# Squared-ReLU MLP after an attention layer: two phases through DRAM, with a seven-product (Strassen) first matmul, float32

## The chip, the cores and the metric

One core of a Trainium2 chip runs the whole program. The metric is the device time of one execution in microseconds (us); lower is better. The core's engines are TensorE (PE; its weight loads are shown apart as PEld), VectorE (DVE), ScalarE (ACT), GpSimd (POOL) and SyncE (SP). SP and POOL also issue the transfers between DRAM and the on-chip memory (SBUF); matmul results land in eight PSUM banks of 128 partitions by 512 float32.

## The reference

One layer: an attention mixer and then an MLP, on 2048 tokens of width 1024, all float32. The change concerns the MLP alone:

```
x = x + g_m * fox_mixer(h, ...)                       # attention, 16 heads
h = rms_norm(x, norm_mlp) * (1 + sc_f) + sh_f         # h: 2048 x 1024
x = x + g_f * (square(relu(h @ w_mlp_in)) @ w_mlp_out) # 1024 -> 4096 -> 1024
```

## The kernel before

Every float32 product is made of three matmuls on a split of each operand into a high and a low part: `mm3` (L132 to L134) adds hi·hi, hi·lo and lo·hi into one bank. A weight or activation that came from DRAM is therefore split before use: ACT casts it to the high part, DVE subtracts that from the raw tile for the low part. A matmul has 128 x 128 weights and 512 moving columns.

The attention, with the out-projection of the first five row tiles (`early_out`) running beside it, ends at about 1480 us; the instructions up to there are the same in both kernels. Then `out_project` handles row tiles 5 to 15 (a row tile is 128 tokens): 48 matmuls into two banks `py`, `ty` = py x gate on DVE (L784), added to x on POOL (L785), stored as x1 by POOL's queue (L786), and its sum of squares taken on ACT (L788). When four row tiles (512 tokens, a block j) are complete, `mlp_norm` makes their rstd (`rstd_of`, L121 to L127: small operations on DVE, Ln and Exp on ACT) and scales the rows, and `mlp_transpose` transposes them on PE (`xt`, L799), applies the modulation on ACT (L801), splits the result on DVE (L803, L804) and, for blocks 1 to 3, stores it to h2_d. These steps are interleaved as side work of the matmul loops.

The MLP is a loop over the four blocks j. Each block goes through eight chunks of four column blocks fb (128 of the 4096 hidden units each). For each fb: load 512 KB of w1 (L876, SP queue) and split it (L864, L865), 24 matmuls into `pu`, ReLU on ACT (L886), square on POOL (L887), split of the result `a` (L889, L890), load 512 KB of w2 and split it. After four fb: 96 matmuls `my` in eight banks of four products each, each bank copied or added to `ya` in SBUF by DVE (L907, L915). In the last chunk of a block DVE multiplies by the second gate and adds (L910, L911), after POOL has multiplied `ya` by the gate and added x1 (L899, L900). So every block reads all of w1 and w2 again, and the hidden activations never leave SBUF.

Where an engine's order matters: each engine, and SP's queue of transfers, works through its instructions in one fixed order. An instruction whose inputs are not ready holds everything behind it on that engine. The program text is not that order: a scheduler interleaves the engines' lists when the program is built.

Of the kernel before, what the change touches and what calls it, by code (L numbers as in the profile page):

```python
# [56 lines left out]
def fox_layer(ctx, tc, x, c, norm_mix, norm_mlp, w_ada, b_ada, w_mlp_in, w_mlp_out,  # L58
# [17 lines left out]
    h2_d = [[dram.tile([P, 2, TJ], F32, name=f"h2_d{j}_{k}") if j else None for k in range(KB)] for j in range(NJ)]  # L76
# [37 lines left out]
    modf = con.tile([P, 2, KB], F32, name="modf")  # L114

# [27 lines left out]
    pw, wo, wo_stage = None, [], []  # L143

# [30 lines left out]
    with ExitStack() as st:  # L175
# [521 lines left out]
        for n, (need, dp) in enumerate(attention()):  # L697
# [29 lines left out]
    sb = ctx.enter_context(tc.tile_pool(name="p2", bufs=2, reuse_waits="tile"))  # L727

    def ring(tag, shape, dt, nm):
        if tag == "w":  # L730
            return pw.tile(shape, dt, tag=tag, name=nm, bufs=8)
        return sb.tile(shape, dt, tag=tag, name=nm,
                       bufs={"raw": 4, "h": 8, "a": 8, "ya": 2, "s": 4, "g": 2}[tag])

    xj, ssj = {}, {}

    def open_x(j):
        xj[j] = ring("ya", [P, RB, D], F32, f"x2_{j}")
        ssj[j] = sb.tile([P, RB], F32, tag="ss", name=f"ss2_{j}", bufs=2)

    def early_load(i):
        j, t = divmod(i, RB)
        nc.sync.dma_start(xj[j][:, t, :], x1_d[i])
        jk = ring("s", [P, D], BF16, f"jk2_{i}")
        nc.scalar.activation(jk, xj[j][:, t, :], AF.Square, accum_out=ssj[j][:, t:t + 1])

    ots = {}

    def out_fetch(i):
        j, t = divmod(i, RB)  # L750
        if t == 0:
            open_x(j)
        ots[i] = ring("raw", [P, D], F32, f"o2_{i}")
        nc.sync.dma_start(ots[i], o_d[i])
        nc.sync.dma_start(xj[j][:, t, :], x[i * P:(i + 1) * P, :])

    def out_load(i):

        if i not in ots:
            out_fetch(i)  # L760
        ot = ots.pop(i)
        oT = []
        for hf in range(2):
# [5 lines left out]
            nc.scalar.copy(a[:, 0, :], pt)  # L769
            nc.vector.tensor_tensor(a[:, 1, :], pt, a[:, 0, :].bitcast(F32), op=ALU.subtract)  # L770
            oT += [(a[:, 0, blk[k]], a[:, 1, blk[k]]) for k in range(4)]
        return oT

    def out_project(i, oT, side):
        j, t = divmod(i, RB)
        xt = xj[j][:, t, :]
        for hf, cs in enumerate(halves):
            py = psS.tile([P, TJ], F32, tag="S", name=f"py{i}_{hf}")
            for kb in range(KB):
                mm3(py, oT[kb], (wo[kb][:, 0, cs], wo[kb][:, 1, cs]), kb == 0, kb == KB - 1)  # L780
                if kb % 4 == 3:
# [29 lines left out]
    h2_first = []

    def load_hT(j):
        hT = []
        for kb in range(KB):
            r = ring("h", [P, 2, TJ], F32R, f"m_h{j}_{kb}")
            nc.sync.dma_start(r.bitcast(F32), h2_d[j][kb])
            hT.append((r[:, 0, :], r[:, 1, :]))
        return hT

    def run(q):
        if q and next(q[0], None) is None and q[0].gi_frame is None:
            q.pop(0)

    side, soon = [], []
    for j in range(NEARLY // RB + (NEARLY % RB > 0)):
        open_x(j)
    oT = out_load(NEARLY)
    out_fetch(NEARLY + 1)
    gates = []  # L830
    for r in range(2):
        g = ring("g", [P, D], F32, f"gate_bc{r}")
        nc.sync.dma_start(g, gate_d[r:r + 1, :].broadcast_to([P, D]))
        gates.append(g)
    gm, gf = gates
# [111 lines left out]
```

## Time and profile before

| | us |
|---|---|
| median of 3 runs (3119.01 to 3124.51) | 3119.08 |
| the profiled execution | 3121.49 |
| span of the profile | 3119.8 |
| PE busy (share of the span) | 2870.4 (92%) |
| DVE busy | 1930.7 (62%) |
| ACT busy | 1433.1 (46%) |
| POOL busy | 1040.5 (33%) |
| mean granted TensorE clock | 0.966 of full speed |
| moved by DMA, mean over the span | 161 GB/s |

The span runs from the first to the last instruction; the profiled execution took 1.7 us more than its span. "Busy" is the time in which an engine executes; the granted clock is the share of TensorE's full speed (2.4 GHz) that it was allowed. Matmuls overlap in the records (each is shown with about 0.4 us, but one starts every 0.23 us), so counts in a stretch say more than their durations.

### The profile page before, as it was taken

What the parts mean: (1) busy time and instruction counts of PE and PEld (TensorE: products, weight loads), DVE (VectorE), ACT (ScalarE), POOL (GpSimd) and SP (SyncE); (2) the same over time, 40 slices, a digit from 0 to 9 for tenths busy, and PEclk for the clock granted to TensorE, in tenths of its full rate; (3) what the DMA queues carried; (4) which work ended last, traced back from release to release, by engine and by line L of the source; (5) the groups of instructions that cost most, each with busy time, mean ns of one, the idle gap of its engine ahead of it and who ended that gap; (6) DMA issues with size and microseconds to landing.
All of it is one profiled execution on the core that took longest, in us unless ns stands there. A gap on an engine that the chain in (4) does not pass through costs nothing.

```text
span 3119.8 us, 44614 instructions
## 1 busy us (share of the span) xinstructions
PE 2870.4 (92%) x16587; PEld 2375.9 (76%) x16587; DVE 1930.7 (62%) x3319; ACT 1433.1 (46%) x2267; POOL 1040.5 (33%) x811
## 2 busy tenths in 40 slices
PE   4788889888988898988999999999999999999999
PEld 4667777777877777776788888788887888878887
DVE  6688978988888877878356433443335333453334
ACT  4466766666676767766233322232222223222321
POOL 3354545545464645445332100410013001311103
PEclk9799989999999999998999999999999999999999
DMA  8479999999999989979755432543235323352332
GB/s 274 124 174 208 208 193 218 209 204 208 213 209 211 201 191 197 189 163 211 215 191 200 132 93 80 172 138 95 75 108 203 94 81 108 95 192 91 108 94 69
DMA packets 852122, 502.34 MB, mean 161 GB/s; under 512 B 585396, under 2 KB 782076, under 8 KB 851904
## 3 DMA queue, kind: packets, MB, share of 16 engines
q1 hardware_dynamic: 843536, 469.60, 62.1%
q0 software_dynamic: 8368, 29.89, 2.5%
q8 instruction: 130, 2.13, 0.3%
q14 instruction: 88, 0.72, 0.1%
HBM read 310.50 MB, written 46.28 MB: 114 GB/s over the span
## 4 chain that ended last, share of the span: by engine, by line
PE 49%; DVE 1%; DMA 1%; ACT 0%; issue 0%; SPq 0%; POOL 0%; DVEq 0%; ACTq 0%
PE my L134 8%; PE my L132 7%; PE my L133 7%; PE pu L134 7%; PE pu L132 7%; PE pu L133 7%; PE py L132 1%; PE py L133 1%; PE py L134 1%; DVE w L865 1%; DMA w1r<-in_w_mlp_in_dram 1%; PE xt L799 0%; PE e_py L132 0%; DMA pT<-ph 0%; PE e_py L134 0%; PE e_py L133 0%
## 5 line engine op out<-in xcount | busy, mean ns | idle before, releaser
L574 DVE SCALAR_TENSOR_TENSOR ph<-L,ph 128x1024 f16<-128x1024 f32 (+7 forms) x384 | 438.3, 1152 | 81.2 <-ACT ph L562 79.5
L887 POOL TENSOR_TENSOR rl<-rl 128x512 f32<-128x512 f32 x128 | 139.1, 1086 | 1024.6 <-ACT rl L886 1019.7
L864 ACT CAST w<-w1r 128x1024 fp32r<-128x1024 f32 x128 | 133.5, 1043 | 598.6 <-PE my L134 553.5
L132 PE MATMUL my<-w,a 128*128 128x512 f32 x1024 | 405.0, 396 | 0.1
L133 PE MATMUL my<-w,a 128*128 128x512 f32 x1024 | 402.9, 394 | 0.0
L134 PE MATMUL my<-w,a 128*128 128x512 f32 x1024 | 395.9, 396 | 2.9 <-DVE a L890 2.9
L562 ACT ACTIVATE ph<-L 128x1024 f16<-128x1024 f32 (+7 forms) x384 | 301.7, 804 | 177.4 <-DMA pT<-ph 152.6
L407 POOL TENSOR_TENSOR hl<-hl,hh 128x1024 fp32r<-128x1024 f32 x120 | 299.5, 2497 | 243.7 <-ACT hh L406 205.4
L487 PE MATMUL psq<-w,hh 128*128 128x384 f32 (+1 forms) x960 | 343.5, 359 | 26.5 <-DVE v L496 12.5
L489 PE MATMUL psq<-w,hl 128*128 128x384 f32 (+1 forms) x960 | 354.4, 371 | 3.2 <-POOL hl L407 2.9
L544 DVE CUSTOM_DVE_ANT_0 L<-S,F 128x1024 f32<-128x1024 f32 (+7 forms) x384 | 343.1, 904 | 19.5 <-PE S L538 6.7
L488 PE MATMUL psq<-w,hh 128*128 128x384 f32 (+1 forms) x960 | 342.7, 359 | 6.1 <-POOL w L333 6.1
L555 ACT ACTIVATE L<-L,st 128x128 f32<-128x128 f32 (+15 forms) x256 | 306.7, 1198 | 89.2 <-DVE st L549 84.9
L537 PE MATMUL S<-kT,qT 128*128 128x512 f32 (+3 forms) x640 | 261.8, 411 | 77.4 <-DVE mx L544 66.6
L600 PE MATMUL po<-v,pT 128*128 128x128 f16 x2176 | 277.1, 228 | 55.4 <-DMA pT<-ph 47.0
L865 DVE TENSOR_TENSOR w<-w1r,w 128x1024 fp32r<-128x1024 f32 x128 | 169.9, 1328 | 236.6 <-ACT w L864 236.6
L915 DVE TENSOR_TENSOR ya<-my,ya 128x512 f32<-128x512 f32 x192 | 128.0, 687 | 292.7 <-PE my L134 292.7
L134 PE MATMUL pu<-m_h,w 128*128 128x512 f32 x768 | 304.4, 396 | 0.0
L132 PE MATMUL pu<-m_h,w 128*128 128x512 f32 x768 | 303.8, 396 | 0.0
L133 PE MATMUL pu<-m_h,w 128*128 128x512 f32 x768 | 301.8, 393 | 0.0
L865 DVE TENSOR_TENSOR w<-w2r,w 128x1024 fp32r<-128x1024 f32 x128 | 165.7, 1295 | 203.7 <-ACT w L864 203.7
L600 PEld LDWEIGHTS <-pT 128*128 128x128 f16 x2176 | 205.1, 103 | 86.2 <-DMA pT<-ph 58.3
(214 smaller groups left out, 6115.8 us busy)
## 6 DMA issues: line engine op xcount, KB each, us to landing
w1r<-in_w_mlp_in_dram SPq DMA_DIRECT2D x128, 512.0 KB
w2r<-in_w_mlp_out_dram SPq DMA_DIRECT2D x128, 512.0 KB
hl<-hT_d SPq DMA_DIRECT2D x120, 512.0 KB
F<-nF_d SPq DMA_DIRECT2D x64, 256.0 KB
wa<-in_w_ada_dram SPq DMA_DIRECT2D x32, 512.0 KB
x<-in_x_dram SPq DMA_DIRECT2D x27, 512.0 KB
wr<-in_fox_w_in_dram SPq DMA_DIRECT2D x64, 192.0 KB
h_d<-h2r POOLq DMA_DIRECT2D x24, 512.0 KB, 3.4
```

The source lines that it names most:

```text
L132: nc.tensor.matmul(ps, lhsT=a[0], rhs=b[0], start=first, stop=False)
L133: nc.tensor.matmul(ps, lhsT=a[0], rhs=b[1], start=False, stop=False)
L134: nc.tensor.matmul(ps, lhsT=a[1], rhs=b[0], start=False, stop=last)
L487: nc.tensor.matmul(ps[:, :n], lhsT=hh, rhs=w[:, 0, :n], start=(kb == 0), stop=False)
L488: nc.tensor.matmul(ps[:, :n], lhsT=hh, rhs=w[:, 1, :n], start=False, stop=False)
L489: nc.tensor.matmul(ps[:, :n], lhsT=hl, rhs=w[:, 0, :n], start=False, stop=(kb == KB - 1))
L544: nc.vector.tensor_tensor_reduce(out=L[:, c0:c1], in0=s2[:, :c1 - c0], in1=Fb[g, h, cch // 2][:, :c1 - c0], scale=1.0, scalar=-3.0e38, op0 ...
L555: nc.scalar.activation(L[:, :W], L[:, :W], AF.Exp, bias=st[:, h:h + 1], scale=1.0, accum_out=st[:, 2 + h:3 + h])
L562: nc.scalar.activation(ph[:, :w], L[:, s0:s0 + w], AF.Copy, scale=PSCALE)
L574: nc.vector.scalar_tensor_tensor(ph[:, w:w + c], L[:, s0:s0 + c], PSCALE, ph[:, :c], op0=ALU.mult, op1=ALU.subtract)
L600: nc.tensor.matmul(po[:, h, :], lhsT=pT[:, bb, :], rhs=v, start=(b == 0), stop=False)
L865: nc.vector.tensor_tensor(w[:, 1, :], raw, w[:, 0, :].bitcast(F32), op=ALU.subtract)
```

## The change

The MLP is done in two phases with the hidden activations written to DRAM in between (a_d), and 1024 tokens (a half s, two blocks j) at a time instead of 512.

Phase 1 computes relu(h @ w1)² in groups of 2x2x2 blocks. A group takes two column blocks (fb = p and p + 16), two halves of the 1024-deep contraction, and two blocks of 512 tokens: eight block products of 4 x 3 matmuls each become seven by Strassen's identity (the Winograd form). The job X of a pair p has the products P1 and P2, the job Y has P6, P7, P5, P4 and P3. The operands of the seven products are sums and differences: of quarters of w1 (S1 to S4, made on POOL by `stage`, L952) and of blocks of h (T1 to T4, made on POOL in `prep_t`, L803 to L810, once for each half s and each of four contraction blocks kk). All are split as before (`split`, L750 on ACT and L751 on DVE; ht0 and ht1 are the raw T1 and T2). The results are combined by DVE additions (`finish`, L980, and `partial`, L987), P1 is first copied out of PSUM by ACT (L999); `finish` then does ReLU on ACT (L981) and the square on POOL (L982), and SP stores the tile (256 KB) to a_d (L1024, L1040). Every operand is prepared three products ahead (LOOK = 3); the first four and the last four X jobs of a half stand together ahead of the four Y jobs.

Phase 2 multiplies a_d by w2: for each half s eight chunks of four fb; a w2 block is loaded (L1069) once for 1024 tokens, the activations are read back (L1075) and split, and 192 matmuls per chunk go to banks that DVE adds to `ya` (L1110 onwards, as before).

Ahead of phase 1, the out-projection now makes the rstd of every row tile by itself (`row_rms`, L756 and L757), transposes only row tiles 0 to 7 (`turn`, from L764), and stores the unsplit h to h2_d by SP's queue; `prep_x` loads and splits the two operands that are not sums (B00, B10). The transposes of the other eight row tiles (with x1 read back, L900) run inside the first half of phase 1. The buffers of the out-projection are given up ahead of phase 1, and those of phase 1 ahead of phase 2, so the new tiles lie in memory that the old ones have used.

```diff
-    for j in range(NJ):
-        hT = load_hT(j) if j > 0 else h2_first
...
+    def row_rms(i, xt):
+        jk = ring("s", [P, D], BF16, f"jk2_{i}")
+        ss = sb.tile([P, 1], F32, tag="ss", name=f"ss2_{i}", bufs=2)
+        nc.scalar.activation(jk, xt, AF.Square, accum_out=ss)
+        nc.vector.tensor_copy(rs2[:, i:i + 1], rstd_of(sb, ss, 1.0 / D, 1, f"x2_{i}"))
...
+    def prep_t(s):
+        for kk in range(KH):
+            b00, b01, b11, b10 = [load_h(s, k, t, kk) for k, t in ((0, 0), (0, 1), (1, 1), (1, 0))]
+            t1, t2 = [ring("hs", [P, TJ], F32, f"ht{n}_{s}_{kk}") for n in range(2)]
+            nc.gpsimd.tensor_tensor(t1, b01, b00, op=ALU.subtract)
+            nc.gpsimd.tensor_tensor(t2, b11, t1, op=ALU.subtract)
+            keep("T2", s, kk, t2)
+            keep("T1", s, kk, t1)
+            yield
+            nc.gpsimd.tensor_tensor(b01, b11, b01, op=ALU.subtract)
+            keep("T3", s, kk, b01)
+            nc.gpsimd.tensor_tensor(b10, b10, t2, op=ALU.subtract)
+            keep("T4", s, kk, b10)
+            keep("B11", s, kk, b11)
+            yield
...
+    RING = {"raw": 8, "w": 5, "st": 5, "p1": 6, "u": 4, "c": 4, "hs": 8}
...
+    PROD = {"P1": ("A00", "B00"), "P2": ("A01", "B10"), "P6": ("S2", "T2"), "P5": ("S1", "T1"),
+            "P7": ("S3", "T3"), "P4": ("A11", "T4"), "P3": ("S4", "B11")}
...
+        if prod == "P6":
+            stage(job, "S1", ALU.add, raw["A10"], raw["A11"])
+            stage(job, "S2", ALU.subtract, job.ops["S1"], raw["A00"])
+            used(job, "A10", "A11", "A00")
+        elif prod == "P7":
+            stage(job, "S3", ALU.subtract, raw["A00"], raw["A10"])
+            stage(job, "S4", ALU.subtract, raw["A01"], job.ops["S2"])
...
+    def finish(job, f, t, ps, other):
+
+        s, p = job.s, job.p
+        c = ring("c", [P, TJ], F32, f"c{f}{t}_{s}_{p}")
+        nc.vector.tensor_tensor(c, ps, other, op=ALU.add)
+        nc.scalar.activation(c, c, AF.Relu)
+        nc.gpsimd.tensor_tensor(c, c, c, op=ALU.mult)
+        late.append((a_d[2 * s + t][p + f * FP], c))
...
+        for kk in range(KH):
+            mm3(ps, (w[:, 0, blk[kk]], w[:, 1, blk[kk]]), hop[b, s, kk], kk == 0, kk == KH - 1)
...
+    for n, (job, prod) in enumerate(slots):
+        while len(late) > 1:
+            nc.sync.dma_start(*late.pop(0))
+        load_jobs()
+        if n + LOOK < len(slots):
+            prepare(*slots[n + LOOK])
+        multiply(job, prod)
+        run(aux)
...
+    for d, c in late:
+        nc.sync.dma_start(d, c)
+    s1x.close()
+    hxx.close()
...
+    RING = {"wr": 2, "ar": 4, "w": 8, "a": 12, "ya": 10, "gf": 1, "x1": 2, "s": 2}
...
+                if t == 0:
+                    wr = ring("wr", [P, D], F32, f"w2r{s}_{fb}")
+                    nc.sync.dma_start(wr, w2[fb * P:(fb + 1) * P, :])
+                    w = ring("w", [P, 2, D], F32R, f"w2_{s}_{fb}")
+                    split(w, wr)
...
+                ar = ring("ar", [P, TJ], F32, f"ar{s}_{fb}_{t}")
+                nc.sync.dma_start(ar, a_d[2 * s + t][fb])
```

The change moves instructions on every engine. Three places follow, each with the rows of one engine in their order (the numbers at the ends of names only tell instances apart; a row's waits are the engines or transfer queues that must have finished something first).

The first is ACT at the end of the out-projection. Before, behind the last row tile's sum of squares (jk2_15), stand casts of weights and the ReLU of a `pu` bank whose matmuls need nothing of that tile; several weight casts stand ahead of it.

```order
L864 CAST w1_0_2_19226<-w1r0_2_19224 128x1024 [waits DMAHW5_49,PE_49]
L864 CAST w2_0_2_19284<-w2r0_2_19282 128x1024 [waits DMAHW6_49,PE_49]
L788 ACTIVATE jk2_15_19125,ss2_3_18653<-x2_3_18652 128x1024 [waits DMAHW0_49,Activation_49,Pool_49]
L864 CAST w1_0_3_19289<-w1r0_3_19287 128x1024 [waits DMAHW7_49,PE_49]
L122 ACTIVATE t_x2_3_19129<-v_x2_3_19127 128x4 [waits DVE_49]
```

Of the change:

```order
L756 ACTIVATE jk2_15_19357,ss2_15_19358<-x2_15_19209 128x1024 [waits DMAHW7_49,Pool_49]
L127 ACTIVATE t_x2_15_19362<-v_x2_15_19360 128x1 [waits DVE_49]
L128 ACTIVATE y_x2_15_19361<-t_x2_15_19362 128x1 [waits Activation_49]
L750 CAST wP1_0_0_19392<-w1_X0_0_A00_19376 128x512 [waits DMAHW6_49,DMAHW2_49,DMAHW0_49]
L750 CAST wP2_0_0_19395<-w1_X0_0_A01_19378 128x512 [waits DMAHW1_49,PE_49]
```

The first weight cast of phase 1 (wP1) now stands behind the whole chain of the last row tile; before, casts of the MLP stood on both sides of it.

The second is POOL at the start of phase 1, of the change (before, POOL had here one square L887 for each fb and nothing else but transfers).

```order
L952 TENSOR_TENSOR S1_0_0_19588<-w1_Y0_0_A10_19401,w1_Y0_0_A11_19403 128x512 [waits DMAHW1_49,DMAHW0_49,PE_49]
L952 TENSOR_TENSOR S2_0_0_19590<-S1_0_0_19588,w1_Y0_0_A00_19405 128x512 [waits DMAHW2_49,Pool_49]
L952 TENSOR_TENSOR S3_0_0_19624<-w1_Y0_0_A00_19405,w1_Y0_0_A10_19401 128x512
L803 TENSOR_TENSOR ht0_0_0_19433<-hr0_01_0_19427,hr0_00_0_19425 128x512 [waits DMAHW4_49,DMAHW3_49]
L982 TENSOR_TENSOR c00_0_0_19461<-c00_0_0_19461 128x512 [waits PE_49,Activation_49]
L952 TENSOR_TENSOR S4_0_0_19626<-w1_Y0_0_A01_19443,S2_0_0_19590 128x512 [waits DMAHW7_49,Pool_49]
L804 TENSOR_TENSOR ht1_0_0_19434<-hr0_11_0_19429,ht0_0_0_19433 128x512 [waits DMAHW5_49,Pool_49]
L808 TENSOR_TENSOR hr0_01_0_19427<-hr0_11_0_19429,hr0_01_0_19427 128x512
L952 TENSOR_TENSOR S1_0_1_19753<-w1_Y0_1_A10_19476,w1_Y0_1_A11_19514 128x512 [waits DMAHW1_49,DMAHW0_49]
L982 TENSOR_TENSOR c00_0_1_19532<-c00_0_1_19532 128x512 [waits Activation_49]
L810 TENSOR_TENSOR hr0_10_0_19431<-hr0_10_0_19431,ht1_0_0_19434 128x512 [waits DMAHW6_49,Pool_49]
```

All sums and differences of w1 and of h and the squares are one list on POOL; from S1 of the first Y job to the last T4 of the first half this list has 29 rows (25 of two inputs, 4 squares).

The third is SP's queue at the start of phase 2, of the change. (Before, the first loads of a chunk stand between other loads, as in the two last rows.)

```order
L1024 DMA a_d3_31_236<-c11_1_15_24950 128x512 [waits DMAHW5_49,Pool_49]
L1040 DMA a_d2_31_204<-c10_1_15_24968 128x512 [waits DMAHW6_49,Pool_49]
L1040 DMA a_d3_15_220<-c01_1_15_24986 128x512 [waits DMAHW7_49,Pool_49]
L1069 DMA w2r0_0_24997<-in_w_mlp_out_dram 128x1024 [waits DMAHW0_49,PE_49]
L1075 DMA ar0_0_0_25002<-a_d0_0_109 128x512 [waits DMAHW1_49]
L1069 DMA w2r0_1_25007<-in_w_mlp_out_dram 128x1024 [waits DMAHW2_49,PE_49]
L1075 DMA ar0_1_0_25012<-a_d0_1_110 128x512 [waits DMAHW3_49,DVE_49]
L1075 DMA ar0_2_0_25022<-a_d0_2_111 128x512 [waits DMAHW4_49]
L1075 DMA ar0_3_0_25032<-a_d0_3_112 128x512 [waits DMAHW5_49]
L1092 DMA gate_bc1_25057<-gate_d_88 128x1024 [waits DMAHW6_49,PE_49]
L1100 DMA m_x1_0_27055<-x1_d0_89 128x1024 [waits DMAHW7_49,PE_49]
L1100 DMA m_x1_1_27102<-x1_d1_90 128x1024 [waits DMAHW0_49]
L1069 DMA w2r0_2_25017<-in_w_mlp_out_dram 128x1024 [waits DMAHW1_49,DVE_49]
```

```order
L893 DMA w2r0_2_19282<-in_w_mlp_out_dram 128x1024 [waits DMAHW6_49,DMAHW2_49,DVE_49]
L876 DMA w1r0_3_19287<-in_w_mlp_in_dram 128x8x128 [waits DMAHW7_49,DMAHW3_49,DVE_49]
```

The first load of w2 stands behind the store of the very last tile of phase 1, which waits for POOL's square; the third load of w2 stands behind the gate and two loads of x1.

## Rows read from the trace of the kernel before

**Rows 1.** Windows: us, PE busy (matmuls started), granted clock, DMA share, GB/s.
```profile
2000.00:2200.00 200.00, 198.89 (x852) 1.00 0.43 140
2400.00:2600.00 200.00, 200.00 (x859) 1.00 0.34 103
3000.00:3120.00 120.00, 114.92 (x493) 0.99 0.25 79
```
**Rows 2.** Waits from 1480 us on: in total us, times, longest us.
```profile
POOL rl L887 <- ACT rl L886: 1019.7, 119, 27.0
ACT w L864 <- PE my L134: 553.5, 31, 17.9
```
**Rows 3.** Lines from 1480 us on: busy us, mean ns; idle before, releaser.
```profile
L134 PE MATMUL my<-w,a 128*128 128x512 f32 x1024 | 395.9, 396 | 2.9 <-DVE a L890 2.9
...
L889 ACT CAST a<-rl 128x512 fp32r<-128x512 f32 x128 | 79.4, 620 | 46.8 <-POOL rl L887 46.8
L886 ACT ACTIVATE rl<-pu 128x512 f32<-128x512 f32 x128 | 76.5, 597 | 372.9 <-PE pu L134 357.5 <-issue 15.4
```
**Rows 4.** One line's instructions: duration ns min/median/max, first and last start us.
```profile
L865 DVE TENSOR_TENSOR w<-w1r,w x128: 1211/1226/3447, 1669.8 to 3072.0; 128x1024 fp32r<-128x1024 f32 x128
...
L890 DVE TENSOR_TENSOR a<-rl,a x128: 675/679/2231, 1685.5 to 3095.0; 128x512 fp32r<-128x512 f32 x128
...
L915 DVE TENSOR_TENSOR ya<-my,ya x192: 679/691/692, 1753.6 to 3070.3; 128x512 f32<-128x512 f32 x192
...
L887 POOL TENSOR_TENSOR rl<-rl x128: 1031/1040/2046, 1682.2 to 3093.2; 128x512 f32<-128x512 f32 x128
...
L785 POOL TENSOR_TENSOR x<-x,ty x22: 1262/1294/1367, 1551.8 to 1675.2; 128x512 f32<-128x512 f32 x22
```
**Rows 5.** Timeline of DVE, 1985 to 2005 us: start us, duration us.
```profile
1991.30 1.22 DVE L865 TENSOR_TENSOR w<-w2r,w 128x1024 fp32r<-128x1024 f32 x1
1992.43 3.45 DVE L865 TENSOR_TENSOR w<-w1r,w 128x1024 fp32r<-128x1024 f32 x1
1995.80 3.43 DVE L865 TENSOR_TENSOR w<-w2r,w 128x1024 fp32r<-128x1024 f32 x1
```
**Rows 6.** Timeline of POOL, the same stretch.
```profile
1991.46 3.33 POOL L899 TENSOR_TENSOR ya<-ya,gate_bc 128x1024 f32<-128x1024 f32 x1 [3.29 <-DVE ya L915]
1994.76 6.75 POOL L900 TENSOR_TENSOR ya<-ya,m_x 128x1024 f32<-128x1024 f32 x2
```
**Rows 7.** Timeline at the end of the out-projection: DVE, POOL, then ACT.
```profile
1674.46 0.68 DVE L784 TENSOR_TENSOR ty<-py,gate_bc 128x512 f32<-128x512 f32 x1
...
1675.22 1.30 POOL L785 TENSOR_TENSOR x<-x,ty 128x512 f32<-128x512 f32 x1 [5.17 <-DVE ty L784]
...
1678.51 1.05 ACT L788 ACTIVATE jk<-x 128x1024 bf16<-128x1024 f32 x1
1679.47 0.19 ACT L788 ACTIVATION_READ_ACCUMULATOR jk<-x 128x1 f32 x1
...
1680.49 0.20 ACT L122 ACTIVATE t_x<-v_x 128x4 f32<-128x4 f32 x1
```
**Rows 8.** Chain that ended last, two of its pieces: start us, us.
```profile
2719.00 0.32 SPq L898
2719.41 5.17 DMA w1r<-in_w_mlp_in_dram
2724.60 1.06 ACT w L864
```
**Rows 9.** DMA issues: count, KB each, median us from issue to landing.
```profile
h_d<-h2r POOLq DMA_DIRECT2D x24, 512.0 KB, 3.4
...
x_d<-x POOLq DMA_DIRECT2D x11, 512.0 KB, 4.0
...
x_d<-wo_raw POOLq DMA_DIRECT2D x5, 256.0 KB, 5.7
```
**Rows 10.** Windows around a wait of PE, columns as in rows 1.
```profile
1464.00:1466.00 2.00, 0.00 (x0) 0.75 1.17 253
1466.00:1468.00 2.00, 1.94 (x17) 0.50 0.72 135
...
1470.00:1472.00 2.00, 2.00 (x9) 0.54 0.95 257
```
**Rows 11.** Timeline of PE behind that wait.
```profile
1466.06 0.29 PE L600 MATMUL po<-v,pT 128*128 128x128 f16 x1 [3.13 <-DMA pT<-ph]
```

More of the change, by code (lines that the diff above doesn't have):

```diff
@@ L741, in early_load @@
[L741 to L755 removed]
+    NS = NJ // 2
@@ L811, in fox_layer, with early_load @@
[L811 to L823, printed above, removed]
+        row_rms(i, xt)
+    def early_load(i):
+        xt = ring("xe", [P, D], F32, f"x2_{i}")
+        nc.sync.dma_start(xt, x1_d[i])
+        row_rms(i, xt)
+        return turn(i, lambda hf: xt[:, halves[hf]])
@@ L825, in fox_layer, with held_x @@
+    def held_x(xt):
+        return lambda hf: xt[:, halves[hf]]
+    NA = 2 * RB
     side, soon = [], []
[L826 to L828 removed]
+    nxt = out_load(NEARLY)
     out_fetch(NEARLY + 1)
[L830 to L835, printed above, removed]
+    gm = ring("gm", [P, D], F32, "gate_bc0")
@@ L850, in fox_layer, with ring @@
-    side += soon
+        if i < NA:
+            soon.append(turn(i, held_x(xt)))
+        if i == NA:
+            soon.append(prep_x(0))
+    while side:
+        run(side)
+    px.close()
+    pwx.close()
+    s1x = ctx.enter_context(ExitStack())
+    sb = s1x.enter_context(tc.tile_pool(name="p3", bufs=2, reuse_waits="tile"))
+    RING = {"raw": 8, "w": 5, "st": 5, "p1": 6, "u": 4, "c": 4, "hs": 8}
+    RING["hx"] = RING["hs"]
+    def ring(tag, shape, dt, nm):
+        tag = "hs" if tag == "hx" else tag
+        return sb.tile(shape, dt, tag=tag, name=nm, bufs=RING[tag])
@@ new lines, in fox_layer @@
+    LOOK = 3
+    aux = [prep_t(0)] + [turn(i, reload_x(i)) for i in range(NA, NT)]
+    n_last_x = max(n for n, (job, prod) in enumerate(slots) if job.s == 0 and job.kind == "X")
+    n_last_y = max(n for n, (job, prod) in enumerate(slots) if job.s == 0)
+    load_jobs()
+    for n in range(LOOK):
+        prepare(*slots[n])
+    for n, (job, prod) in enumerate(slots):
+        while len(late) > 1:
+            nc.sync.dma_start(*late.pop(0))
+        load_jobs()
+        if n + LOOK < len(slots):
+            prepare(*slots[n + LOOK])
+        multiply(job, prod)
+        run(aux)
+        if n == n_last_x:
+            aux.append(prep_x(1))
+        if n == n_last_y:
+            while aux:
+                run(aux)
+            aux.append(prep_t(1))
+        if n == 2 * Q - 1:
+            while len(aux) > NT - NA:
+                run(aux)
```

313 lines of the change are left out of this document (209 added, 104 removed).

## Prediction

> **What bounds the kernel now.** I read the windows first. From 2000 us on PE is busy practically all the time at full clock [rows 1]; in the fullest window 859 matmuls start in 200.00 us, one every 232.8 ns. That pitch, not the 0.396 us that a record shows [rows 3], is the price of a matmul here. Next the waits: the long ones are other engines waiting for each other or for PE, such as POOL for ReLU, 1019.7 us, or ACT for `my`, 553.5 us [rows 2]. PE itself lost 2.9 us behind `my` [rows 3], and a few us where a block j begins, visible as 198.89 of 200. So in the MLP only the number of matmuls counts, as long as operands come in time, and fewer matmuls shorten the program nearly one to one.
>
> **What is removed.** The first product had 4 x 32 x 24 = 3072 matmuls `pu`; now there are 2 halves x 16 pairs x 7 products x 12 = 2688. The second keeps its 3072, and the transposes keep their number. Saved: 384 x 232.8 ns = **89.4 us**. The waits at `my` inside the fused loop go too, 2.9 us. Together **-92.3 us**.
>
> Beside this goes a check of whether PE stays the bound. A pair of jobs (X and Y) has 84 matmuls, 84 x 0.2328 = 19.56 us. DVE has seven subtractions of 0.68 (as L890) and seven additions out of PSUM of 0.69 (as L915) [rows 4], 9.6 us. POOL has four sums of two inputs at 1.29 (as L785) and four squares at 1.04 (as L887) [rows 4], 9.3 us. ACT has seven casts of 0.62, four ReLU of 0.60 [rows 3] and one copy, about 7.3 us. DMA moves six loads and four stores of 256 KB, 2.5 MB, 134 GB/s over the pair, where the MLP already saw 140 [rows 1]. Each fits under 19.56.
>
> DVE and POOL do not run freely beside each other: a subtraction L865, 1.22 us, took 3.45 and 3.43 while POOL ran L899 and L900 [rows 5], and these took 3.33 and 3.4 [rows 6]; each starts where the other ends. Additions from PSUM (L915) never stretch, maximum 692 ns [rows 4]. So I let POOL and the seven DVE subtractions exclude each other: 9.3 + 4.8 = 14.1 us of 19.56. Steady state stays with PE. The Trainium skill, page "SBUF — State Buffer", section "Who interferes with whom", says that a DVE instruction with two SBUF inputs and a GpSimd instruction that reads SBUF share one port as an exclusive lock, and that DVE with one SBUF input does not contend; it speaks against a change that adds POOL sums, and rows 4 to 6 agree with it.
>
> The Trainium skill, page "TensorE: Matmul & The Clock Gate", section "Wait — 56ns, not 53.3ns?", gives 215.7 ns from start to start at 512 columns; with it the saving would be 82.8 us. The trace's 232.8 ns decides.
>
> **What is added, all of it at the seams.** Before, PE always had matmuls of another kind to go on with. Now three dependencies run through everything.
>
> (A) Out-projection. Each row tile makes its own rstd, about nine small operations where four tiles shared one set, and `run(side)` comes twice as often. Nothing of PE's next tile hangs on it; 0 to 3 us, nearest to nothing: **1**.
>
> (B) Start of phase 1. Once the last `py` is done, wP1 stands on ACT behind the last tile's chain (the first place in the order): `ty` 0.68, POOL's sum 1.30, sum of squares 1.05 + 0.19, one small DVE step, Ln and Exp at 0.20 each [rows 7], then the cast 0.62 [rows 3]: 4.2 us and some 1 us of handovers, 5.3. Before, the matmuls of `pu` covered this. Then PE has eight X products (96 matmuls, 22.3 us) and what the first Y job offers as T operands arrive (60, 14 us, and transposes, 1.8): 38 us of work until T4 of the last kk. POOL's list to there has 25 x 1.26 to 1.29 + 4 x 1.04 = 36 us. It starts late: SP sends the loads of h only after all X and three Y quarters of w1, and the Y quarters reuse tiles that the first splits must free, so about 7 us after the last `py`, plus a landing of 3.4 to 5.7 us [rows 9] for the first difference: at 11. The ring of eight tiles for h lets the loads of kk = 2 and 3 start only when DVE has read older ones: 2 to 3 us idle. So T4 is ready at 50 to 53 us if DVE never shuts POOL out, at up to 68 with full exclusion (some 25 splits of 0.68 fall into the stretch). PE needs it at 5.3 + 38 = 43. Bubble: 5.3 + (8 to 25), that is 13 to 31 us, to 36 with loads as slow as 5.7 each time. Exclusion was seen, so I take the upper middle, **27**.
>
> (C) From the first half to the second. The T operands of the second half go into the buffers of the first, so prep_t(1) comes only behind its last Y product. Cover are the four X jobs ahead, 8 x 2.79 = 22 us; POOL must do about 19 operations, 24 us, plus splits, and the loads. 0 to 12 us; the POOL work alone ends about when the cover does, so I take **6**.
>
> (D) From phase 1 to phase 2. The first w2 load on SP stands behind the last store of a_d (third place): after the last matmul DVE 0.69, ReLU 0.60, square 1.04, handovers: 2.6 us. Then a load of 512 KB, 5.17 us, and its cast, 1.06 [rows 8], the cast of a, 0.62: PE restarts at about 9.4. Then w2 of block 2 stands behind the gate and two x1 loads, in a ring of two, so PE pauses again; below, the second pause vanishes (8 us in all); above, it costs two loads (18). I take **12**.
>
> (E) Clock. After PE had waited 3.13 us [rows 11] the granted clock was 0.50 until about 1472 us [rows 10], some 5.6 us at 1.2 instead of 2.4 GHz, a loss of 2.8. Seams B and D are longer gaps: 2 x 2.8 = **6** (0 to 8).
>
> (F) Small waits in steady state and the last chunk, where POOL multiplies 16 tiles against DVE: 0 to 6, **1**. The end behind the last matmul is the same as before.
>
> Phase 2 costs nothing else: a chunk has 192 matmuls, 44.7 us, against DVE 4 x 1.22 + 8 x 0.68 + 16 x 0.69 = 21.4 us and 4.2 MB of DMA, 94 GB/s.
>
> Sum: -92.3 + 1 + 27 + 6 + 12 + 6 + 1 = **-39 us**. The profiled execution took 3121.5, so 3082; the median of runs lies 2.4 us lower, so I predict **3080 us**. With all low ends (0 + 13 + 0 + 8 + 0 + 0 = 21) it is 3048, with all high ends (3 + 36 + 12 + 18 + 8 + 6 = 83) 3110.
>
> **Rivals.**
> 1. The seams are cheap: T operands keep up (PE's order interleaves the four products as they arrive), C is covered, D restarts once. Costs 21 to 35, time **3048 to 3062**. For it: POOL's bare list (36 us) is shorter than PE's cover. Against: in-order loads and the exclusion of rows 5 and 6. Chance 0.22.
> 2. The seams are long: every stage waits for a load in turn, B and C together 48 or more, D 18, clock 8. Costs 68 to 90, time **3095 to 3117**. For it: SP is one queue. Against: an issue takes SP 0.32 us [rows 8], so loads can be under way side by side. Chance 0.2.
> 3. Slower: the pair's chain of waits sets the pace in phase 1. A product's operand must pass a load, POOL's sum, cast and subtraction within three products, 8.4 us; S1, S2, cast and subtraction alone take 2 x 1.29 + 0.62 + 0.68 = 3.9, and squares queued on POOL and stores on SP stand in between. If PE waits in each pair, 32 pairs multiply it: from 19.56 + 39/32 = 20.8 us a pair on, the gain is gone; at 22 us it is 32 x 2.4 = 78 us more, **3158**. For it: POOL's list mixes squares that wait for PE with sums that PE waits for. Against: 14.1 of 19.56 us of work, 4.5 us of slack in a product's lead. Chance 0.08.
> 4. The program does not have the fewer matmuls or PE's pitch changes. Its order shows 2688; the shapes are the same. Chance below 0.02, put to rival 3.
>
> **Numbers.** Forecast (3062 to 3095) 0.5, rivals 0.22, 0.2, 0.08. The range 3047 to 3111 leaves out the tail of rival 2 and rival 3, and a little below rival 1: about 0.15. A measurement of this kernel tells 0.2 per cent, 6 us, from no change, so faster means below 3112.8: 0.5 + 0.22 + 0.16 = 0.88; same 0.04; slower 0.08.
>
> **What would show it.** Right: 2688 matmuls of the first product at 232.8 ns; PE with three visible gaps, where phase 1 starts, at its half, and where phase 2 starts, of about 32, 6 and 15 us with their clocks at 0.50; between them PE at 99 per cent or more; POOL nearly without idle time in the first 50 us of phase 1; DVE subtractions stretched beside POOL. Wrong: PE idle in every pair (rival 3), or PE waiting there for loads of w1 rather than for T operands (rival 2), or gaps that sum to under 25 us (rival 1).

## The result, and the profile after

| | before | after |
|---|---|---|
| median of 4 runs, us | 3121.80 (3119.01 to 3124.51) | 3043.84 (3041.05 to 3048.27) |
| ratio, 95% interval | | 0.9752 (0.9733 to 0.9770) |
| profiled execution, its span, us | 3121.49, 3119.8 | 3046.07, 3044.4 |
| PE / DVE / ACT / POOL busy, us | 2870 / 1931 / 1433 / 1041 | 2760 / 2078 / 1460 / 1257 |
| matmuls of the first product | 3072 | 2688 |

Faster by 78 us (the 3121.80 are the 3119.08 of the table ahead of the prediction with a fourth run); forecast were 3080 us and a range from 3047 to 3111. The time lies 3 us below the range and 36 below the forecast.

The windows of the kernel after (columns as in rows 1), first two stretches in the middle of the phases, then the seams:

```profile
1900.00:2000.00 100.00, 100.00 (x442) 1.00 0.48 153
2400.00:2600.00 200.00, 200.00 (x884) 1.00 0.28 90
...
1670.50:1740.00 69.50, 54.50 (x179) 0.80 0.57 173
1740.00:2015.00 275.00, 273.83 (x1232) 1.00 0.57 177
2015.00:2045.00 30.00, 22.05 (x81) 0.83 0.54 170
2045.00:2331.90 286.90, 286.90 (x1268) 1.00 0.40 126
2331.90:2350.00 18.10, 10.05 (x35) 0.72 0.84 307
```

The second line is the surprise. In 200 us with PE full and its clock at 1.00 now 884 matmuls start; before, 859 [rows 1]. The `my` matmuls, 3072 of the same shape in both kernels, start every 226.7 ns instead of every 233.3 (the mean over sequences without a gap; the prediction's 232.8 came from dividing 200 us by a count that takes in the matmuls at both edges). This is no wait that has gone: PE was full in both.

The waits of PE from 1660 us on, after (us in total, times, longest us), are the seams that were forecast:

```profile
PE my L137 <- ACT a L750: 8.1, 1, 8.1
PE mP L137 <- DVE c L980: 5.3, 1, 5.3
PE mP L137 <- ACT T L750: 4.7, 4, 2.9
PE mP L137 <- ACT wP L750: 4.5, 1, 4.5
PE mP L138 <- DVE T L751: 3.1, 6, 1.2
PE mP L137 <- ACT p L999: 2.6, 1, 2.6
PE mP L139 <- DVE wP L751: 1.9, 1, 1.9
```

The gaps in PE's timeline after (in brackets: idle before, releaser) tell where three of them stand: start of phase 1, its half, phase 2.

```profile
1675.36 0.50 PE L137 MATMUL mP<-B,wP 128*128 128x512 f32 x1 [4.54 <-ACT wP L750]
...
2033.57 0.80 PE L137 MATMUL mP<-B,wP 128*128 128x512 f32 x1 [5.32 <-DVE c L980]
...
2340.33 2.07 PE L137 MATMUL my<-w,a 128*128 128x512 f32 x4 [8.05 <-ACT a L750]
```

DVE and then POOL of the kernel after, in the first of them (start us, duration us). A subtraction of two SBUF tiles takes 0.68 us by itself [rows 4], a POOL sum 1.27; here they take 1.6 to 1.8. Their records overlap, so a duration contains waiting: a subtraction ends 0.54 to 0.55 us behind the end of a POOL record (1703.07 to 1703.61, 1699.66 to 1700.21), a POOL sum 1.14 to 1.15 us behind the end of a subtraction (1700.21 to 1701.36, 1703.61 to 1704.75). They work in turn. An addition that reads PSUM (L980) keeps its 0.68:

```profile
1698.45 1.76 DVE L751 TENSOR_TENSOR T<-hr,T 128x512 fp32r<-128x512 f32 x1
1700.13 0.68 DVE L980 TENSOR_TENSOR c<-mP,p 128x512 f32<-128x512 f32 x1
...
1702.02 1.59 DVE L751 TENSOR_TENSOR T<-hr,T 128x512 fp32r<-128x512 f32 x1
1703.53 1.77 DVE L751 TENSOR_TENSOR B<-hr,B 128x512 fp32r<-128x512 f32 x1
```

```profile
1697.94 1.72 POOL L810 TENSOR_TENSOR hr<-hr,ht 128x512 f32<-128x512 f32 x1
1699.62 1.74 POOL L952 TENSOR_TENSOR S<-S,w_Y_A 128x512 f32<-128x512 f32 x1
1701.32 1.75 POOL L952 TENSOR_TENSOR S<-w_Y_A,w_Y_A 128x512 f32<-128x512 f32 x1
1703.02 1.73 POOL L803 TENSOR_TENSOR ht<-hr,hr 128x512 f32<-128x512 f32 x1
```

So the account was nearly right, and beside it something had happened that was not in the account: all matmuls of the MLP had become 6.7 ns shorter, 5760 x 6.67 = 38 us.

What could that be? The matmuls of the out-projection (py), of the same shape, still started every 233.5 ns in the kernel after, so neither the chip nor the execution was faster. One of its sequences, 94 steps in 21.95 us:

```profile
1648.48 0.41 PE L138 MATMUL py<-wo,oT 128*128 128x512 f32 x1
...
1670.43 0.39 PE L139 MATMUL py<-wo,oT 128*128 128x512 f32 x1
```

The shapes, the types and the program around a matmul are the same. The tiles had moved, though. The address of a tile within its partition is fixed when the program is built, and it is read from the built program; the traces don't show it. Before, w1, w2 and wo lay at 224 modulo 256 bytes, hT at 64, the activations at 128; after, every operand of the MLP lies at 128. The theory was that the address of the operands sets the pitch, that is, the time from one matmul's start to the next one's. The rivals: the place in memory or PSUM, something in the two-phase order, or the chip.

### The profile page after: what moved, and what is told of

Same layout as the page of the kernel before. It is cut to its first block, busy times and chain, and to the rows that moved or that the text cites. A ratio compares the mean times of both kernels' runs of the same rounds, so it can differ in the third digit from the quotient of the medians.

```text
span 3044.4 us, 45983 instructions
## 1 busy us (share of the span) xinstructions
PE 2760.2 (91%) x16203; PEld 2306.8 (76%) x16203; DVE 2078.0 (68%) x3659; ACT 1460.2 (48%) x2507; POOL 1256.7 (41%) x947
## 5 line engine op out<-in xcount | busy, mean ns | idle before, releaser
L606 PE MATMUL po<-v,pT 128*128 128x128 f16 x2176 | 276.5, 228 | 69.5 <-DMA pT<-ph 61.1
L543 PE MATMUL S<-kT,qT 128*128 128x512 f32 (+3 forms) x640 | 262.3, 411 | 71.0 <-DVE mx L550 62.0
L606 PEld LDWEIGHTS <-pT 128*128 128x128 f16 x2176 | 204.7, 103 | 100.2 <-DMA pT<-ph 71.9
L1101 POOL TENSOR_TENSOR ya<-ya,gate_bc 128x1024 f32<-128x1024 f32 x16 | 41.1, 2572 | 546.2 <-DVE ya L1118 546.1
L607 PE MATMUL po<-v,pT 128*128 128x64 f16 x2176 | 258.7, 200 | 0.0
L544 PE MATMUL S<-kT,qT 128*128 128x512 f32 (+3 forms) x640 | 241.1, 384 | 0.0
L137 PEld LDWEIGHTS my<-w,a 128*128 128x128 f32 x1024 | 192.8, 188 | 49.1 <-ACT a L750 8.5
L607 PEld LDWEIGHTS <-pT 128*128 128x128 f16 x2176 | 197.7, 101 | 42.6 <-issue 31.7
L750 ACT CAST w<-w2r 128x1024 fp32r<-128x1024 f32 x64 | 67.3, 1051 | 336.3 <-PE my L139 264.0
L138 PEld LDWEIGHTS my<-w,a 128*128 128x128 f32 x1024 | 193.0, 188 | 40.2
```

The source lines that it names most:

```text
L137: nc.tensor.matmul(ps, lhsT=a[0], rhs=b[0], start=first, stop=False)
L138: nc.tensor.matmul(ps, lhsT=a[0], rhs=b[1], start=False, stop=False)
L606: nc.tensor.matmul(po[:, h, :], lhsT=pT[:, bb, :], rhs=v, start=(b == 0), stop=False)
L607: nc.tensor.matmul(po[:, h, 0:HD], lhsT=pT[:, nw + bb, :], rhs=v[:, 0:HD], start=False, stop=(b == nb - 1))
```

## The experiments

Where an unused tile is put in, everything behind it moves up in memory; the instructions stay the same. In experiments 1 to 7 this is the only edit (4 to 6 also clear one unused tile). Of experiments 1, 2, 3 and 7 there is one execution each, so there the pitches count and not the totals; of the others there are four.

**1. One operand off.** The T operands, B11 and, in phase 2, the activations move by 32 bytes:

```diff
+            once(sb, "T")
             w = sb.tile([P, 2, TJ], F32R, tag="hT", name=f"{name}_{s}_{kk}", bufs=5 * KH)
...
+                once(sb, "A4")
                 a = ring("a", [P, 2, TJ], F32R, f"a{s}_{fb}_{t}")
```

`once` allocates an unused tile of the given size (here 32 bytes in a partition) at its first call and nothing afterwards.

> The changed kernel with empty gaps in the on-chip memory: in phase 1 the T operands and B11 (moving, 28 of 28 kilobytes of the Y job's operands) lie 32 bytes off a multiple of 128, the weights and B00, B10 on it; in phase 2 the activations (weights of the matmul) lie 32 bytes off, w2 on it. Theory (the start-to-start time of a 512-column matmul depends on the address of its operands: 226.7 ns when both are multiples of 64 bytes, 233.3 ns when one is not): X products stay at 226.7 ns, Y products go to 233.3, `my` to 233.3; time 3044 + (1920 + 3072) x 6.67 ns = 3077 us. Rival 1 (the place in memory, the PSUM bank or the chip sets it, not the alignment): 226.7 everywhere, 3044 us. Rival 2 (only the moving operand's address counts): Y 233.3, `my` 226.7, 3057 us.

Measured: 3072.7 us. X products stay at 226.7 ns, but for the first eight or so behind a Y job, which are mixed; Y products go to 233.2, `my` to 233.3. Within one execution a run of X products is followed by Y products (PE's timeline, starts 0.226 and then 0.233 us apart):

```profile
1901.08 0.39 PE L137 MATMUL mP<-B,wP 128*128 128x512 f32 x1
...
1904.25 0.39 PE L139 MATMUL mP<-B,wP 128*128 128x512 f32 x1
1904.48 0.40 PE L137 MATMUL mP<-T,wP 128*128 128x512 f32 x1
...
1911.48 0.39 PE L137 MATMUL mP<-T,wP 128*128 128x512 f32 x1
```

14 steps from 1901.08 to 1904.25 are 226.4 ns each, 30 steps from 1904.48 to 1911.48 are 233.3. The place and the chip as rivals are out (32 bytes do it, and both pitches stand in one execution), and so is rival 2, since `my` got slow by its weights alone.

**2. Both off, with other gaps** (32 bytes ahead of B00, ahead of the weights of phase 1, and ahead of both operands of phase 2).

> As the run before it, with other gaps: in phase 1 the weights lie 32 bytes off, B00 and B10 too, the T operands on a multiple of 128; in phase 2 both operands lie 32 bytes off. Theory (each operand counts by itself): X, Y and `my` all at 233.3 ns, 3044 + 5760 x 6.67 ns = 3082 us. Rival 1 (place, not alignment): 226.7 everywhere, 3044 us. Rival 3 (only the two operands' offset from one another counts): X and `my` at 226.7, Y at 233.3, 3057 us. The e_py matmuls of both traces (both operands 32 bytes off a multiple of 64, at 232.2 and 228.9 ns) speak for something between.

Measured: 3083.9 us, X, Y and `my` at 233.3 to 233.4. As the first theory said; but the gaps had put the operands at 160 and 32 modulo 256, not on the same offset, so rival 3 was not yet tested. The window of `my`, against 884 in the kernel after:

```profile
2460.00:2660.00 200.00, 200.00 (x859) 1.00 0.30 99
```

**3. Gaps of 64.**

> As the run before it, with gaps of 64 bytes: in phase 1 the weights lie 64 bytes off a multiple of 128, B00 and B10 too, the T operands on it; in phase 2 w2 (moving) lies 64 bytes off, the activations on it. Theory with a grain of 64 bytes: 226.7 ns everywhere, 3044 us. With a grain of 128 bytes: X, Y and `my` at 233.3, 3082 us.

Measured: 3075.6 us, Y 229.2, `my` 233.3. Both grains fail: there are more than two values. Y has moving at 128 and weights at 64; e_py, which was at 229.3 in the kernel after, has 224 and 160, the same distance.

**4. The kernel before, moved.** 96 bytes at the upper end of memory, so that w1, w2 and wo go from 224 to 128 modulo 256:

```diff
+                    padR = ctx.enter_context(tc.tile_pool(name="padR", bufs=1, side="right"))
+                    nc.vector.memset(padR.tile([P, 24], F32, name="pad_R"), 0.0)
                     pw = ctx.enter_context(tc.tile_pool(name="pw", bufs=2, reuse_waits="tile", side="right"))
```

> The kernel before with one edit: an unused 96-byte tile at the upper end of the on-chip memory, so that the weights of w1, w2 and wo, which lay 32 bytes off a multiple of 64, lie on a multiple of 128 (the activations and hT already lie on multiples of 64). Nothing else changes. Theory: `pu`, `my` and `py` at 226.7 ns, 3121.8 - (6144 + 528) x 6.67 ns = 3077 us. Rival 1 (the faster matmuls came from the two phases or from where the new tiles lie): no change, 3122 us, pitch 233.3.

Measured: 3097.3 us, ratio to before 0.9941 (0.9923 to 0.9959), where 3077 was expected. `my` fell to 226.9 and py to 228.5, but `pu` (hT at 64, weights at 128) stayed at 233.3. Half of it, as only one of the two products of the MLP had got operands at the same offset.

**5. The kernel before, all at 128.** The same and 64 bytes ahead of hT.

> The kernel before with the 96-byte gap at the upper end (as in the aligned run before it) and a 64-byte gap ahead of the hT tiles, so that both operands of `pu`, `my` and `py` lie on multiples of 128 bytes. Theory, with the grain corrected to 128 bytes: `pu` goes from 233.3 to 226.7 ns too, 3072 x 6.67 ns = 20.5 us less than the aligned run before it (3097.3), 3077 us; then the change proper, with equal alignment, is worth only 3077 - 3044 = 33 us. Rival (what matters is the rest modulo 512, which was equal, 384, in all fast cases; here hT lies at 128 of 512 and the weights at 384): `pu` stays at 233.3, 3097 us.

Measured: 3083.7 us, ratio 0.9874 (0.9854 to 0.9895), `pu` at 226.7 too. The window of `my` and `pu` in this kernel, against the 859 of rows 1:

```profile
2460.00:2660.00 200.00, 200.00 (x884) 1.00 0.33 100
```

The kernel before, run beside it, took 3119.8, which is 4 us more than beside experiment 4; the rest of the 7 us above the 3077 expected is not explained. So 36 us, against the change's 78, are to be had in the kernel before by two empty gaps, without any of its 384 matmuls less. hT at 128 and weights at 384 modulo 512 are as good as equal, so the period is no longer than 256 bytes.

**6. The kernel after with attention and out-projection moved** (96 bytes at both ends).

> The changed kernel with gaps of 96 bytes at both ends, so that the operands of the attention's and out-projection's matmuls lie on multiples of 128 (some of 64, for head slices) as well; the MLP's lie there already. Theory: py and e_py fall from 233.4 and 229.3 to 226.7 ns, 528 x 6.7 + 240 x 2.6 ns = 4 us; in the attention, where PE is busy 0.87 of the time, 0 to 10 us more; 3030 to 3040 us. Rival (alignment acts only on the MLP's tiles): 3044 us.

Measured: 3026.7 us, ratio to before 0.9694 (0.9674 to 0.9714), 17 us less than the change and below the range expected. py fell to 228 ns (its long sequences to 226.7): from its first matmul to its last it took 136.1 instead of 138.9 us (136.1 again in the two versions below, 138.9 in experiment 9). But e_py went up, from 229.3 to 232.6, with wo at 128 and its weights at 0 modulo 256: multiples of 128, and yet slow. That speaks against "multiples of 128" and for a distance. So only 2 to 3 of the 17 us can be laid to the pitch. Most of the rest was gained ahead of the MLP: the first e_py stands at 1408.8 us, in the kernel after at 1418.8. All four runs (3018.9 to 3030.6) lie below the four of the change, so this is no chance of one execution. The two versions at the end, whose gap at the lower end is 192 bytes instead of 64, did not have it (1419.6 and 1420.4). What made the attention shorter here stays open.

**7. Distance or multiple.** Gaps that set the two readings against each other: Y at 160 and 160, X at 224 and 160, `my` at 0 and 128.

> The changed kernel with other gaps, to tell two readings of the fast pitch apart. Reading A: both operands must lie on multiples of 128 bytes. Reading B: only the distance of the two operands counts, modulo 256 bytes: 0 gives 226.7 ns, 64 gives 229.3, other distances up to 233.3. Here the Y products have both operands at 160 of 256 (off every multiple of 64, distance 0), the X products 224 and 160 (distance 64), `my` has w2 at 0 and the activations at 128 (both on multiples of 128, distance 128). By A: X and Y 233.3, `my` 226.7 ns, time 3044 + 2688 x 6.67 ns = 3062 us. By B: X (two of seven products) 229.3, Y 226.7, `my` 233.3 ns, 3044 + 768 x 2.6 ns + 3072 x 6.67 ns = 3066 us; the times lie close, the pitches tell.

Measured: 3066.4 us; Y 227.8 ns with its sequences at 226.7, X 229.2 (with B11, which has Y's distance), `my` 232.4. Reading B in all three, but for `my`, which is 1 ns under its 233.3; reading A in none. In its timeline the first ten or so Y products behind an X product are mixed (226 to 234), the following ones run at 226.7, which is why Y's mean is not 226.7; why the switch takes that long is open. One run of Y products, both operands at 160, 47 steps of 226.8 ns, and then the window of `my` (0 and 128, 862 where the kernel after has 884):

```profile
1975.51 0.39 PE L137 MATMUL mP<-T,wP 128*128 128x512 f32 x1
...
1986.17 0.39 PE L139 MATMUL mP<-T,wP 128*128 128x512 f32 x1
...
2460.00:2660.00 200.00, 200.00 (x862) 1.00 0.31 103
```

What was measured, by the distance (address of the moving operand less that of the weights, modulo 256 bytes):

| distance | moving, weights (kernel, matmul) | ns from start to start |
|---|---|---|
| 0 | 128, 128 (after, mP and `my`; experiment 5, `pu`); 160, 160 (7, Y) | 226.7; 227.8 |
| 32 | 160, 128 (1, Y) | 233.2 |
| 64 | 128, 64 (3, Y); 224, 160 (after, e_py; 7, X) | 229.2; 229.3; 229.2 |
| 96 | 224, 128 (before, `my`); 64, 224 (before, `pu`); 128, 32 (2, Y) | 233.3; 233.3; 233.4 |
| 128 | 160, 32 (2, `my`); 0, 128 (7, `my`); 224, 96 (before, e_py); 128, 0 (6, e_py) | 233.3; 232.4; 232.1; 232.6 |
| 192 | 192, 0 (3, `my`); 64, 128 (4, `pu`) | 233.3; 233.3 |
| 224 | 128, 160 (1, `my`) | 233.3 |

**8. Two phases without the seven products.** Eight products in the same order, two in one bank, no sums on POOL and no DVE additions:

```diff
-        slots += [(job, prod) for prod in (("P1", "P2") if job.kind == "X" else ("P6", "P7", "P5", "P4", "P3"))]
+        slots += [(job, prod) for prod in (("00a", "00b") if job.kind == "X" else ("10a", "10b", "11a", "11b", "01a", "01b"))]
...
+            c = ring("c", [P, TJ], F32, f"c{f}{t}_{s}_{p}")
+            nc.scalar.activation(c, ps, AF.Relu)
+            nc.gpsimd.tensor_tensor(c, c, c, op=ALU.mult)
```

> The changed kernel without the seven-product identity: phase 1 makes each 2x2x2 group with eight products (two accumulate in one bank, no sums on POOL, no additions on DVE, ReLU straight from PSUM); two phases through DRAM, halves of 1024 tokens, loads and stores as they are, all operands on multiples of 128 bytes. 3072 matmuls in phase 1 instead of 2688. Theory: 384 x 226.7 ns = 87 us more, less the seams that the sums cause (some 15 to 25 us at the start of phase 1 and at its half): 3106 to 3116 us; so two phases alone, against the kernel before with equal alignment (3077), cost about 30 to 40 us. Rival (the identity gives little, as the sums' cost eats it): under 3080 us.

Measured: 3094.0 us, ratio 0.9913 (0.9898 to 0.9928). From the last py to the last `my` it takes 1416.9 us, against 1403.0 in experiment 5 and 1368.7 in the kernel after. So two phases alone cost 14 us, less than half of the 30 to 40 that I had expected; the identity gives 48 of its 87 us. PE's waits in this kernel: the two seams that have nothing to do with sums are there in full, those at T operands and at the half of phase 1 are gone.

```profile
PE my L137 <- ACT a L750: 7.8, 1, 7.8
PE m00a L137 <- ACT wA L750: 4.5, 1, 4.5
PE m00a L139 <- DVE wA L751: 0.4, 1, 0.4
```

**9. The T subtractions on DVE.**

```diff
-            nc.gpsimd.tensor_tensor(t1, b01, b00, op=ALU.subtract)
+            nc.vector.tensor_tensor(t1, b01, b00, op=ALU.subtract)
```

(and the three others of `prep_t`)

> The changed kernel with the 16 subtractions of each half that make T1 to T4 on DVE instead of POOL; nothing else. Theory (at the start of phase 1 the POOL sums and the DVE subtractions of two SBUF inputs exclude each other, and their joint list, 29 x 1.25 + 27 x 0.68 = 54 us, sets when PE has its operands): the list becomes 16 x 0.58 = 9 us shorter, PE's gap there falls from 27 to about 16 us, with the clock's half-speed stretch shorter by some us: 3030 to 3036 us. Rival 1 (the loads of h, in order on SP, set it): no change, 3044. Rival 2 (DVE becomes the late engine, since it now carries subtractions and splits): up to 10 us slower, 3054.

Measured: 3028.1 us, ratio to before 0.9700 (0.9685 to 0.9716); from the last py to the last `my` 1355.1 instead of 1368.7 us, 14 less. So the joint list of POOL and DVE set the length of these seams, and neither rival came. But at the start of phase 1 PE's gap did not fall from 27 to 16 us, as expected. In the 70 us there PE is idle for 15.0 us in the kernel after and for 13.9 here (a wait of 4.7 us for the copy of P1 has taken the place of some at operands). What changed is the clock: in windows of 5 us it was 0.50 from 1710 to 1730 us in the kernel after, and here 0.72 and 0.59 from 1710 to 1720 us and 1.00 behind that. So 217 matmuls start instead of 181 (the kernel after first):

```profile
1670.00:1740.00 70.00, 55.00 (x181) 0.80 0.56 172
...
1663.00:1733.00 70.00, 56.11 (x217) 0.90 0.65 199
```

With the loads as they are, moving work from the slower of the two to the one that takes half as long per operation helps, though DVE has more to do.

**10. Put together, S on POOL**, and **11. with S on DVE.** Gaps that put out-projection and e_py at distance 0, T on DVE (in 11 S1 to S4, too), and, so that the first loads of w2 don't stand behind other transfers:

```diff
-            nc.sync.dma_start(*late.pop(0))
+            (nc.sync if n < len(slots) - 3 else nc.gpsimd).dma_start(*late.pop(0))
...
     for d, c in late:
-        nc.sync.dma_start(d, c)
+        nc.gpsimd.dma_start(d, c)
...
-            nc.sync.dma_start(gf, gate_d[1:2, :].broadcast_to([P, D]))
+            nc.gpsimd.dma_start(gf, gate_d[1:2, :].broadcast_to([P, D]))
...
-                nc.sync.dma_start(x1, x1_d[i])
+                nc.gpsimd.dma_start(x1, x1_d[i])
```

> A version put together: the changed kernel with the gaps of the run in which attention and out-projection lie on multiples of 128 (here with e_oT at 128 of 256, as wo), the T subtractions on DVE, the last three stores of a_d, the gate and the x1 loads on POOL's queue instead of SP's, so that the first loads of w2 do not stand behind them. S1 to S4 stay on POOL. Theory (terms add): 3026.7 - 16 (T on DVE, from 3044 to 3028) - 8 to 10 (the gap of PE where phase 2 starts, 8.1 us and its clock) = 3000 to 3004 us. Rival 1 (the gap at phase 2 is set by the last `finish` itself, not by SP's order): 3010 us. Rival 2 (POOL's own transfers delay its squares): slower than 3010.

Measured: 3025.2 us, 0.9696 (0.9673 to 0.9719). A miss of more than 20 us: the terms did not add. From the last py on it takes 1352.9 us, only 2 less than with T on DVE alone. The start of phase 2 did shrink: SP's order was its cause.

```profile
2316.78 0.39 PE L139 MATMUL mP<-B,wP 128*128 128x512 f32 x1
2320.12 1.22 PE L137 MATMUL my<-w,a 128*128 128x512 f32 x2 [2.96 <-ACT a L758]
```

2.96 us where there were 8.05. But phase 1 took 2.7 us more than in experiment 9, and the 17 us of experiment 6 had contained its shorter attention, which did not come with these gaps.

> As the run before it, with S1 to S4 on DVE too, so that POOL has the squares alone. Theory (POOL sums and DVE subtractions share a path, and a sum takes 0.68 us on DVE against 1.27 on POOL): the start of phase 1 becomes a few us shorter still, 2995 to 3002 us; steady state has DVE at 7 x 0.68 + 7 x 0.69 + 4 x 0.68 = 12.3 of 19 us and stays with PE. Rival (DVE in order: additions that free PSUM banks stand behind sums that wait for loads, and PE waits in every pair): 3005 to 3060 us.

Measured: 3019.2 us, 0.9673 (0.9651 to 0.9696), the fastest kernel of all: 102.6 us below the 3121.8 of before, 24.6 below the change. It is still 17 us above the range expected, which started from the same sum. From the last py on it takes 1347.8 us, 5 less than with S on POOL. The time lies in the rival's range, but what the rival says (PE waits in every pair) did not come: in steady state PE is full.

```profile
1860.00:1960.00 100.00, 100.00 (x443) 1.00 0.46 148
```

## Why the prediction was wrong, point by point

**The step that failed** stands in "what bounds the kernel now" and again in rival 4: the pitch of 232.8 ns was taken as "the price of a matmul here", carried over to tiles that lie elsewhere, and "PE's pitch changes" was dismissed with "the shapes are the same". The shapes were; the addresses were not. It fell by 6.67 ns for 5760 matmuls, 38.4 us. Experiment 2, the changed kernel with the old pitch everywhere, gives 3083.9 us, where 3080 was forecast; 3043.8 + 38.4 gives 3082.

**Removed matmuls:** 384 of them, 2688 left, as forecast: 384 x 233.3 = 89.6 us, forecast 89.4. Beside that 2.9 us of waits.

**Added at the seams**, forecast 53 us, measured 55 by counting starts in the windows above against 0.2267 us for a matmul and 0.1 for a transpose (in the kernel before, eight take 0.79 us until the next matmul starts). That the sums agree is luck, as below:

| | forecast | measured |
|---|---|---|
| (B) start of phase 1, with its part of the clock (E) | 27 + 3 | 69.5 - 169 x 0.2267 - 1 = 30 |
| (C) half of phase 1 | 6 | 30.0 - 81 x 0.2267 = 12 |
| (D) start of phase 2, with its part of (E) | 12 + 3 | 18.1 - 35 x 0.2267 = 10 |
| (A), (F) and steady state | 2 | 275 - 1176 x 0.2267 - 5.6 = 3 |
| sum | 53 | 55 |

The parts do not agree. PE's idle time, window less busy time in the result's table of windows, is 15.0 us at (B), 8.0 at (C) and 8.1 at (D), 31 together, where 27 + 6 + 12 = 45 were forecast. The other 21 of the 52 us at these three seams (15, 4 and 2) went into matmuls that ran at a granted clock below 1.00 (mean 0.80, 0.83 and 0.72 in these windows); (E) had 6. The gaps were put 14 us too long and the clock 15 us too low, and the two errors cancel. (E) took 2.8 us for a seam, from one gap of 3.13 us; a seam with many short gaps costs more, and (C), which (E) left out, had its share.

(B) had its cause right: PE waited 4.5 us at wP1, as written, and in 11 gaps of under 3 us for T operands and one weight tile, and experiment 9 shows that POOL's and DVE's list sets its length. The last T4 sum ended 58.5 us behind the last py (1728.9 less 1670.4), between the 50 and 68 forecast. But most of what PE lost to it came as slow matmuls: between 1710 and 1730 us the clock was 0.50.

```profile
1705.00:1710.00 5.00, 0.51 (x1) 0.19 (x1) 3.43 (x4) 1.04 (x2) 5.00 (x4) 1.00 0.64 194
1710.00:1715.00 5.00, 4.48 (x8) 2.40 (x9) 4.22 (x3) 1.34 (x3) 5.00 (x4) 0.50 0.75 232
...
1725.00:1730.00 5.00, 4.34 (x11) 2.54 (x11) 4.48 (x5) 2.75 (x6) 3.93 (x3) 0.50 0.33 100
```

(The columns are PE, PEld, DVE, ACT and POOL busy, then the clock, DMA share and GB/s; POOL is full until 1715 us.)

(C) was taken too low, and its mechanism was not the forecast one. X products had their operands; what they lacked was a free bank. The addition that empties it (L980) stood on DVE behind splits of T operands that POOL held up:

```profile
2028.28 1.52 DVE L751 TENSOR_TENSOR wP<-w_X_A,wP 128x512 fp32r<-128x512 f32 x1
2029.72 1.52 DVE L751 TENSOR_TENSOR T<-hr,T 128x512 fp32r<-128x512 f32 x1
2031.17 1.74 DVE L751 TENSOR_TENSOR B<-hr,B 128x512 fp32r<-128x512 f32 x1
2032.84 0.68 DVE L980 TENSOR_TENSOR c<-mP,p 128x512 f32<-128x512 f32 x1
```

(D) had the cause right (SP's order: 2.96 us in experiment 10 instead of 8.05). The second pause behind the gate and x1 was not there: PE waited 0.2 us for w2 later on.

**Rivals.** 1 (cheap seams) would have given nearly the right time (3048 to 3062) for the wrong reason: the seams cost 55 us, not 21 to 35. 2 (loads in turn, 68 us or more) did not come either: PE's waits name T operands, banks and the two first casts, not loads of w1. 3 (a pace set by the pair's chain) did not come: between the seams 1268 matmuls start in 286.90 us. That DVE and POOL exclude each other was read rightly, but not "each starts where the other ends": in rows 5 and 6, too, L865 of 1992.43 starts while POOL's L899 runs, and ends 1.1 us behind it. The Trainium skill, page "SBUF — State Buffer", section "Who interferes with whom", has it as an exclusive lock for two SBUF inputs, and the trace agrees in both halves, 1.6 to 1.8 us for L751 beside POOL, 0.68 for L980. The Trainium skill, page "TensorE: Matmul & The Clock Gate", section "Wait — 56ns, not 53.3ns?", gives 215.7 ns at 512 columns; no run here reaches it, the lowest is 226.7.

## What to carry to other kernels

Where PE is full, compare the number of matmuls that start in a window before and after: busy time and clock looked the same here, and the count told of 38 us. Before a rewrite, look at the addresses of what is multiplied: with moving operand and weights at the same offset modulo 256 bytes float32 matmuls of 512 columns ran 3% faster in every stage tried, for two empty gaps. Measure other widths first (below). When a change moves tiles, price the unchanged instructions again, too; and consider giving sums of two SBUF tiles to DVE rather than to POOL when DVE subtracts beside it, as experiments 9 and 11 did here.

## What the runs showed of the hardware

The start-to-start time of these float32 matmuls (128 x 128 weights, 512 columns) depends on the distance between the addresses of moving operand and weights in a partition: 226.7 ns at 0 modulo 256 bytes, 229 at 64, 232 to 233.4 at 32, 96, 128, 192 and 224. Neither operand's own alignment decides it (160 and 160 is fast, 0 and 128 is slow). A distance of 160 was not tried, and what in the memory causes it stays open; it was not seen whether the weights of the same or of the next matmul count, as their offsets are equal.

The rule did not hold for the 384 columns of the attention. There, in the kernel after, matmuls `psq`<-w,hh and w,hl of 384 columns lie at four distances (order and addresses from the built program, starts from the trace), and those that follow one another without a gap start 176.5 ns apart at 0, 175.1 at 64, 175.5 at 128 and 172.2 at 192 (means of 258 to 674 steps; the kernel before gives the same within 0.3 ns): 0 is not the best there. Whether addresses made the attention of experiment 6 shorter is not shown either: the first e_py, which starts beside the attention's last part, stands at 1409 us there and between 1416 and 1425 in all other runs.
